# A conditioned decoder block on one core: the opening's w_ada in two sets, and the second norm in the order of need

## The chip, the core and the metric

The kernel runs on one core of one Trainium2 chip. A core has a matrix engine (TensorE, in the profile PE, with its weight loads as PEld), a vector engine (VectorE, DVE), a scalar engine (ScalarE, ACT), GpSimd (POOL) and a queue engine (SyncE, SP) that issues most DMAs here. The metric is the time of one execution on the device in microseconds (us), lower is better; the time before is the median of three runs.

## The reference

One decoder block on 256 tokens of width 2048, all in 32-bit floats. A condition vector `c` is turned by a large matrix `w_ada` (2048 x 12288) into six modulation vectors; two of them shift and scale the first norm, two the second one. Three matter here:

```python
mod = c_act @ w_ada[l] + b_ada[l]
sh1, sc1, g1, sh2, sc2, g2 = [m[:, None, :] for m in jnp.split(mod, N_MOD, axis=-1)]
h = rms_norm(x, norm_mix_g[l]) * (1.0 + sc1) + sh1
proj = h @ w_in[l]                       # u, q, k, v, ga, gb
...
x = x + g1 * (merged @ w_out[l])
h2 = rms_norm(x, norm_mlp_g[l]) * (1.0 + sc2) + sh2
x = x + g2 * (jnp.square(jax.nn.relu(h2 @ w_ff1[l])) @ w_ff2[l])
return rms_norm(x, norm_final_g)
```

Between `proj` and `merged` lie a state-space branch and an attention branch, which the change doesn't touch.

## The kernel before

**Products in three parts.** Each large product is made from split operands: a 32-bit value is cast to a shorter form (`hi`, on ACT) and the rest of it (`lo = src - hi`, on DVE) is kept beside it; three matrix products (hi x hi, hi x lo, lo x hi) are added up. `split` (lines 135 to 142) emits the cast and the subtraction and notes both in `self.done`, as a pair (subtraction, cast). It is used for the weights, which come through `stream`, and for the activations.

**The weight stream.** `stream` (lines 143 to 156) loads one tile of 128 rows and 1024 columns (512 KB) into one of seven buffers `wraw`, splits it into `whi` and `wlo`, and hands it to the product. A buffer comes free when the subtraction has read it; SP's next load hangs on that. The same seven buffers serve the tiles of `w_ada`: `ada_first` (lines 275 to 305) multiplies such tiles on PE, with outputs named `adap` and `adac`, for the first columns of the two vectors of the first norm, and `ada_job` (lines 307 to 329) multiplies them on DVE (line 323, called a modulation job here) for all others.

**Queues and order.** A planner places the instructions on each engine's queue by a priority and a simulated time line; each queue then runs strictly in its order. `high_priority` lifts what is written inside it, `hot()` most of all; `issue_after(i)`, here `after(i)`, puts what follows behind the instruction `i` on the same engine; `pin` keeps the order of the program. `self.gates` is a list of pairs: each next weight tile of the stream takes one from it, and its subtraction goes behind the first of the pair, its cast behind the second.

**The opening.** The first norm's activations `ah` and `al` are made in pairs of 128-row blocks by `make_h1` (line 419): a multiplication by the norm on DVE, scale and shift on ACT into `htmp`, then a split. The first product (`gemm_t`, line 158, for the query columns) runs over four weight rows, 0 to 3; rows 0 and 1 need the first pair of `ah`, rows 2 and 3 the second. The second pair needs its own columns of `w_ada`: four tiles for the scale, four for the shift, which `second` (line 929) loads and multiplies. It is called as `mid` from `gemm_t` in front of row 2, so that on PE all eight totals stand behind row 1. Each set of four ends in a round trip: PE `adap`, ACT copy, PE `adac`, a small DVE sum.

**The second norm.** The output projection runs by `gemm_h` (line 219): its second column half first finishes the tokens 0 to 127 (half 0), then the held products for the tokens 128 to 255 (half 1). As each half is done, `norm2` (line 1176) runs: `add1` adds the product to the residual on DVE (line 1159 and 1160) and squares it on ACT; then come the sum, `rstd` (a square root on ACT and small DVE steps), `scale2` for two column blocks (DVE, line 1172), and for each block four transposes on PE (line 1190, output `trh`), scale and shift on ACT (line 1194, into the one buffer `htmp`), and a split into `mh` and `ml`. All of it is in `hot()`.

The next product, the first of `w_ff1` (call of `gemm_h` at line 1293), has eight weight tiles, 0 to 7; tiles 0 to 3 use block 0 of the norm, tiles 4 to 7 block 1. Tiles 0 to 3 lie in `whi` and `wlo`, 4 and 5 in `wVT`, 6 and 7 in `wQT`. It takes half 0 through all eight tiles, and then half 1. The list `turns=(((6, 3),), ())` puts the products of half 0 from tile 6 on behind `self.turned[3]`, the last transpose of half 1. The gates of the eight tiles are

```python
self.gates = [(None, None)] + [(scaled[0], None)] * 2 + [(scaled[0], roots[0])] * 3 + [(h0, roots[0])] * 2
```

with `scaled[t]` the first `scale2` of half t, `roots[t]` its square root and `h0` the subtraction of half 0's second block. Behind this product six modulation jobs are forced, after `h1` (the last subtraction of half 1); the others are handed out at a rate `RM` for each step of a weight stream, over three further groups of eight steps.

Of the kernel before, what the change touches and what calls it, by code (L numbers as in the profile page):

```python
# [55 lines left out]
RSS = .43  # L56
RPA = .65
RWO = .45
RM = .45
NP = 4  # L60
TW = 9
TF = 3
# [12 lines left out]
class Kern:  # L75
# [82 lines left out]
    def gemm_t(self, src, kts, c0, xh, xl, koff=0, mid=None):  # L158
        nc = self.nc
        banks = [self.bank(f"pt{b}") for b in range(4)]  # L160
        n = len(kts)
        for i, (kt, hi, lo) in enumerate(self.stream(src, kts, c0)):
            kx = kt - koff
            if mid and i == n // 2:
                mid()
            for blk in range(8):
                o = banks[blk // 2][:, (blk % 2) * S:(blk % 2 + 1) * S]
                c = slice(blk * P, (blk + 1) * P)
                st, sp = i == 0 and blk % 2 == 0, i == n - 1
                nc.tensor.matmul(o, hi[:, c], xh[:, kx, :], start=st, stop=False, skip_group_check=True)  # L170
                nc.tensor.matmul(o, hi[:, c], xl[:, kx, :], start=False, stop=False, skip_group_check=True)  # L171
                self.mm = nc.tensor.matmul(o, lo[:, c], xh[:, kx, :], start=False, stop=sp, skip_group_check=True)  # L172
        return banks
# [101 lines left out]
    def ada_first(self, j, half, done):  # L275
        nc = self.nc
        n = 2 * (1 - j) + half
        st = {}

        def load(i):  # L280
            w = st[i] = self.wp.tile([P, 1024], F32, name="wraw", tag="wraw", bufs=7)
            with self.after(self.last):
                ld = nc.sync.dma_start(w, self.a["wan"][j, half, i])
            if self.early:
                self.last = ld

        def total(i):
            w = st.pop(i).rearrange("p (k n) -> p k n", k=4)
            if i == 0:
                st["p"] = self.aux("adap")  # L290
            p = st["p"][:, 0:256]
            with self.after(None if self.early else self.mm):
                for k in range(4):
                    q = 32 * k
                    nc.tensor.matmul(p[q:q + 32, :], self.cz[:, 4 * i + k, :], w[:, k, :], start=i == 0,
                                     stop=i == 3, tile_position=(0, q), skip_group_check=True)
# [555 lines left out]
    def body(self):  # L852
# [73 lines left out]
            self.ssm_params()  # L926
            self.bias_prep()

        def second():
            with self.tc.high_priority(offset=OF1):  # L930
                for ld, tot in modn(1):
                    ld()
                    tot()
                self.make_h1(range(2, 4), A1, B1)
        self.early = False
        self.qk = self.slot("S1", [P, 2, 8, S], name="qk")
        self.v = self.slot("SV", [P, 2, 1024], name="v")
# [64 lines left out]

        def qkvu(which, g0, g1):
            kts = range(groups[g0][0], sum(groups[g1]))
            mid = second if (which, g0) == (0, 0) else (lambda: need(g1)) if g1 > g0 else None
            need(g0)
            if which < 2:
                qk_evac(which, self.gemm_t(win, kts, 1024 + 1024 * which, self.ah, self.al, mid=mid), g0)
            elif which == 2:
                v_evac(self.gemm_n(win, kts, 3072, self.ah, self.al), g0)  # L1010
            elif which == 4:
                g_evac(self.gemm_t(win, kts, 4096, self.ah, self.al, mid=mid), g0)
            else:
                u_evac(self.gemm_t(win, kts, 0, self.ah, self.al), g0)
# [127 lines left out]
        for cg in range(2):  # L1142
# [11 lines left out]
            def add1(t):  # L1154
                with self.hot():
                    for b in (2 * t, 2 * t + 1):
                        c = slice(cg * 1024 + (b % 2) * 512, cg * 1024 + (b % 2) * 512 + 512)
                        tmp = xs[:, t, c]
                        self.pin(v.tensor_mul(tmp, banks[b], g1t["t"][:, c]))
                        self.pin(v.tensor_add(x1[:, t, c], x1[:, t, c], tmp))  # L1160
                        nc.scalar.activation(tmp, x1[:, t, c], AF.Square,
                                             accum_out=sq[:, t * 4 + cg * 2 + b % 2:t * 4 + cg * 2 + b % 2 + 1])

            if cg == 0:
# [8 lines left out]

        scaled, roots = {}, {}

        def norm2(t):
            add1(t)
            with self.hot():
                ss = self.col(f"ss2{t}", 1)
                self.pin(v.reduce_sum(ss, sq[:, 4 * t:4 * t + 4], axis=AX.X))  # L1180
                rs2[t] = self.rstd(ss, 1, f"r2{t}")
                roots[t] = self.sq_last
                tk = slice(t * P, (t + 1) * P)
                scaled[t] = [scale2(c, t) for c in range(2)][0]
                for c in range(2):
                    p = self.tmp("trh")
                    h = self.big.tile([P, 4, P], F32, name="htmp", tag="htmp", bufs=1)
                    for k in range(4):
                        kt = 4 * c + k
                        self.turned[2 * t + c] = nc.tensor.transpose(  # L1190
                            p[:, k * P:(k + 1) * P], xs[:, t, kt * P:(kt + 1) * P], self.ident)
                    for k in range(4):
                        kt = 4 * c + k
                        nc.scalar.activation(h[:, k], p[:, k * P:(k + 1) * P], AF.Identity,
                                             scale=A2[:, kt:kt + 1], bias=B2[:, kt:kt + 1])
                    last = self.split(mh[:, 4 * c:4 * c + 4, tk], ml[:, 4 * c:4 * c + 4, tk], h)
            return last

        h0 = norm2(0)
        next(parts)  # L1200
        h1 = norm2(1)
        self.gates = [(None, None)] + [(scaled[0], None)] * 2 + [(scaled[0], roots[0])] * 3 + [(h0, roots[0])] * 2

        g2b = self.slot("S3", [P, D], name="g2b")

# [84 lines left out]
        for g in range(NP):  # L1290
            part = self.slot(("S4", "T", "SV", "S5")[g], [P, 8, S], name="part")
            if g == 0:
                halves = self.gemm_h(w1, range(0, 8), 0, mh, ml, self.homes(4, ("VT", "QT")), 8,
                                     turns=(((6, 3),), ()))
                for t in range(2):
                    banks = next(halves)
                    for b in (2 * t, 2 * t + 1):
# [7 lines left out]
            if g == 0:  # L1305
                self.gates = []
                self.agate = h1
                for job in range(6):
                    if self.lanes["ada"][0]:
                        self.lanes["ada"][0].pop(0)()  # L1310
                self.agate = None
# [65 lines left out]
```

## Time and profile before

| what | us |
|---|---|
| median of 3 runs | 1417.61 (1416.76 to 1420.15) |
| profiled execution | 1415.01 |
| its span, first to last instruction | 1412.9 |
| PE idle in the span | 42.1 |

The span is read from the profile, in which each time is counted from the span's start. A row of the timeline gives start, duration, engine, line, operation, output<-inputs, shape and count, and in brackets how long the engine was idle before it and what ended that. Matrix products are pipelined, so one starts before the one ahead of it has ended.

### The profile page before, as it was taken

How to read it: one execution, taken by the hardware profiler on the slowest of the kernel's cores; microseconds unless marked ns; L12 is line 12 of the kernel's file. 1: busy time of each engine (PE TensorE's matmuls, PEld its weight loads, DVE VectorE, ACT ScalarE, POOL GpSimd, SP SyncE). 2: the span in 40 equal slices, each digit the busy share in tenths (PEclk: the TensorE clock that was granted, in tenths of full speed). 3: DMA queues.
4: the chain of work that ended last, by engine and by line, in shares of the span. 5: the costliest groups of instructions: out<-in, count | busy, mean ns of one | idle time of the engine just before them, and what ended most of it. 6: DMA issues, size and time to landing. Idle time of an engine off the chain costs nothing. (4 is left out here: it accounts for less than half of the span.)

```text
span 1412.9 us, 23391 instructions
## 1 busy us (share of the span) xinstructions
PE 1370.8 (97%) x9258; PEld 1221.4 (86%) x9258; DVE 1054.7 (75%) x1502; ACT 705.7 (50%) x937; POOL 40.8 (3%) x94
## 2 busy tenths in 40 slices
PE   7889999999999999999899999999999999999996
PEld 5779899899999999988788888888888888888885
DVE  5688989986799888978786776777676555555676
ACT  4444343366464843445555564545463544635444
POOL 1000000320000300000000000000000000000000
PEclk9999999999999999999999999999999999999998
DMA  9999987597457988797597677777767556465551
GB/s 340 368 381 351 327 295 243 164 296 243 150 190 250 320 305 294 285 349 283 181 324 262 196 263 242 246 251 278 255 221 265 184 191 195 174 203 192 182 205 60
DMA packets 113293, 353.19 MB, mean 250 GB/s; under 512 B 12080, under 2 KB 12096, under 8 KB 113056
## 3 DMA queue, kind: packets, MB, share of 16 engines
q1 hardware_dynamic: 110384, 347.13, 70.6%
q0 software_dynamic: 2800, 4.58, 1.1%
q8 instruction: 72, 1.18, 0.3%
q14 instruction: 37, 0.30, 0.1%
HBM read 347.27 MB, written 2.29 MB: 247 GB/s over the span
## 5 line engine op out<-in xcount | busy, mean ns | idle before, releaser
L137 ACT CAST whi<-wraw 128x1024 fp32r<-128x1024 f32 x443 | 461.3, 1051 | 550.8 <-PE pn L268 173.4
L139 DVE TENSOR_TENSOR wlo<-wraw,whi 128x1024 fp32r<-128x1024 f32 x443 | 537.7, 1222 | 256.0 <-ACT whi L137 254.2
L198 PE MATMUL pw<-mh,whi 128*128 128x512 f32 x896 | 311.3, 396 | 1.0 <-DVE part L1303 0.5
L170 PE MATMUL pt<-ah,whi 128*128 128x256 f32 x896 | 252.0, 288 | 9.9 <-ACT whi L137 6.8
L171 PE MATMUL pt<-ah,whi 128*128 128x256 f32 x896 | 250.8, 286 | 0.0
L200 PE MATMUL pw<-mh,wlo 128*128 128x256 f32 x896 | 242.4, 280 | 0.0
L172 PE MATMUL pt<-ah,wlo 128*128 128x256 f32 x896 | 238.7, 285 | 2.7 <-DVE wlo L139 2.5
L323 DVE SCALAR_TENSOR_TENSOR wraw<-wraw,cb 128x1024 f32<-128x1024 f32 x176 | 213.3, 1219 | 0.0
L268 PE MATMUL pn<-whi,ff 128*128 128x512 f32 x512 | 199.3, 389 | 0.0
L267 PE MATMUL pn<-whi,ff 128*128 128x512 f32 x512 | 198.6, 390 | 0.0
L198 PEld LDWEIGHTS pw<-mh,whi 128*128 128x128 f32 x896 | 165.4, 188 | 37.3 <-DVE part L1303 0.8
L269 PE MATMUL pn<-wlo,ff 128*128 128x512 f32 x512 | 185.3, 389 | 0.0
L170 PEld LDWEIGHTS pt<-ah,whi 128*128 128x128 f32 x896 | 172.5, 194 | 13.3 <-ACT whi L137 8.7
L171 PEld LDWEIGHTS pt<-ah,whi 128*128 128x128 f32 x896 | 173.2, 194 | 0.4
L200 PEld LDWEIGHTS pw<-mh,wlo 128*128 128x128 f32 x896 | 168.8, 188 | 4.7 <-DVE wlo L139 0.4
L172 PEld LDWEIGHTS pt<-ah,wlo 128*128 128x128 f32 x896 | 165.5, 193 | 4.2 <-DVE wlo L139 3.9
L267 PEld LDWEIGHTS pn<-whi,ff 128*128 128x128 f32 x512 | 96.1, 188 | 20.1 <-issue 0.2
L269 PEld LDWEIGHTS pn<-wlo,ff 128*128 128x128 f32 x512 | 96.1, 188 | 20.0
L268 PEld LDWEIGHTS pn<-whi,ff 128*128 128x128 f32 x512 | 96.1, 188 | 19.6
L1273 DVE TENSOR_TENSOR y<-y,pn 128x512 f32<-128x512 f32 x48 | 30.8, 682 | 14.9 <-PE pn L269 14.9
L267 PE MATMUL pn<-whi,mh 128*128 128x512 f32 x96 | 37.6, 392 | 0.0
L268 PE MATMUL pn<-whi,mh 128*128 128x512 f32 x96 | 37.4, 390 | 0.0
(400 smaller groups left out, 1655.4 us busy)
## 6 DMA issues: line engine op xcount, KB each, us to landing
wraw<-in_w_ff_dram SPq DMA_DIRECT2D x256, 512.0 KB, 4.7
wraw<-in_wat_dram SPq DMA_DIRECT2D x176, 512.0 KB, 5.8
wraw<-in_w_in_dram SPq DMA_DIRECT2D x128, 512.0 KB, 5.2
wraw<-in_w_out_dram SPq DMA_DIRECT2D x32, 512.0 KB, 6.3
wraw<-in_wan_dram SPq DMA_DIRECT2D x16, 512.0 KB, 8.7
wraw<-in_w_proj_attn_dram SPq DMA_DIRECT2D x16, 512.0 KB, 6.3
wraw<-in_w_proj_ssm_dram SPq DMA_DIRECT2D x16, 512.0 KB, 6.2
wraw<-in_w_glu_dram SPq DMA_DIRECT2D x8, 512.0 KB, 5.5
```

The source lines that it names most:

```text
L137: h = self.nc.scalar.copy(hi, src)
L139: s = self.nc.vector.tensor_sub(lo, src, hi.bitcast(F32))
L170: nc.tensor.matmul(o, hi[:, c], xh[:, kx, :], start=st, stop=False, skip_group_check=True)
L171: nc.tensor.matmul(o, hi[:, c], xl[:, kx, :], start=False, stop=False, skip_group_check=True)
L172: self.mm = nc.tensor.matmul(o, lo[:, c], xh[:, kx, :], start=False, stop=sp, skip_group_check=True)
L198: nc.tensor.matmul(banks[b], hi[:, c], x2[:, k0 + k].rearrange("p h s -> p (h s)"), start=i + k == 0, stop=False, skip_group_check=True)
L200: self.mm = nc.tensor.matmul(banks[b][:, 0:S], lo[:, c], x2[:, k0 + k, 0, :], start=False, stop=i == n - 1 and k == 1, skip_group_check=True)
L267: nc.tensor.matmul(o, xh[:, kx, tk], hi[:, c], start=q == 0, stop=False)
L268: nc.tensor.matmul(o, xl[:, kx, tk], hi[:, c], start=False, stop=False)
L269: self.mm = last = nc.tensor.matmul(o, xh[:, kx, tk], lo[:, c], start=False, stop=q == n - 1)
L323: v.scalar_tensor_tensor(w, w, 1.0, self.cb[:, (i % 2) * 1024:(i % 2 + 1) * 1024], op0=OP.mult, op1=OP.mult, accum_out=pc[:, i:i + 1])
L1273: v.tensor_add(d, d, banks[b])
```

## The change

In the opening, `mid` may now be a dictionary from the row to a function. `second` is called twice: in front of row 1 it loads and multiplies the four tiles of the scale, and row 1's first product of each block goes behind the last of them; in front of row 2 it does the four of the shift and makes the pair. A gate then holds row 3's cast and subtraction behind the pair's. In the second norm, `norm2` is cut in two: its first part goes as far as the eight transposes, and `piece(c)` makes scale, shift and split of one block. Half 0's second block is now written behind half 1's `add1`, by `turn()`. The gates of tiles 5 to 7, the turn (tile 5 in place of 6), the number of forced jobs (four in place of six) and `RM` (0.55 in place of 0.45) change with it.

```diff
-RM = .45
+RM = .55
@@ gemm_t
-            if mid and i == n // 2:
+            turn = None
+            if isinstance(mid, dict):
+                turn = mid[i]() if i in mid else None
+            elif mid and i == n // 2:
                 mid()
...
-                nc.tensor.matmul(o, hi[:, c], xh[:, kx, :], start=st, stop=False, skip_group_check=True)
+                with self.after(turn):
+                    nc.tensor.matmul(o, hi[:, c], xh[:, kx, :], start=st, stop=False, skip_group_check=True)
@@ body
-        def second():
+        rest = modn(1)
+
+        def second(i):
             with self.tc.high_priority(offset=OF1):
-                for ld, tot in modn(1):
+                for ld, tot in rest[4 * i:4 * i + 4]:
                     ld()
                     tot()
+                if i == 0:
+                    return self.adap
                 self.make_h1(range(2, 4), A1, B1)
+                self.gates = self.done[-1:]
...
-            mid = second if (which, g0) == (0, 0) else (lambda: need(g1)) if g1 > g0 else None
+            mid = {1: lambda: second(0), 2: lambda: second(1)} if (which, g0) == (0, 0) else (lambda: need(g1)) if g1 > g0 else None
...
-        def norm2(t):
+        def norm2(t, turn):
             add1(t)
+            turn()
             with self.hot():
                 ss = self.col(f"ss2{t}", 1)
                 self.pin(v.reduce_sum(ss, sq[:, 4 * t:4 * t + 4], axis=AX.X))
                 rs2[t] = self.rstd(ss, 1, f"r2{t}")
                 roots[t] = self.sq_last
+                scaled[t] = [scale2(c, t) for c in range(2)][0]
+                trh = []
+                for c in range(2):
+                    trh.append(self.tmp("trh"))
+                    for k in range(4):
+                        kt = 4 * c + k
+                        self.turned[2 * t + c] = nc.tensor.transpose(
+                            trh[c][:, k * P:(k + 1) * P], xs[:, t, kt * P:(kt + 1) * P], self.ident)
+
+            def piece(c):
...
-        h0 = norm2(0)
+        piece0 = norm2(0, lambda: None)
+        h00 = piece0(0)
         next(parts)
-        h1 = norm2(1)
-        self.gates = [(None, None)] + [(scaled[0], None)] * 2 + [(scaled[0], roots[0])] * 3 + [(h0, roots[0])] * 2
+        h01 = []
+        piece1 = norm2(1, lambda: h01.append(piece0(1)))
+        h01 = h01[0]
+        piece1(0)
+        h1 = piece1(1)[0]
+        self.gates = [(None, None)] + [(scaled[0], None)] * 2 + [(scaled[0], roots[0])] * 2 + [(h01[0], h00[1])]
+        self.gates += [(scaled[1], self.square), (scaled[1], roots[1])]
...
-                                     turns=(((6, 3),), ()))
+                                     turns=(((5, 3),), ()))
...
-                for job in range(6):
+                for job in range(4):
```

`self.square` is the last square of `add1`. `piece(c)` holds the old lines of scale, shift and split for one block and returns `self.done[-1]`, its pair of subtraction and cast.

More of the change, by code (lines that the diff above doesn't have):

```diff
@@ L294, in total @@
                     q = 32 * k
-                    nc.tensor.matmul(p[q:q + 32, :], self.cz[:, 4 * i + k, :], w[:, k, :], start=i == 0,
-                                     stop=i == 3, tile_position=(0, q), skip_group_check=True)
+                    self.adap = nc.tensor.matmul(p[q:q + 32, :], self.cz[:, 4 * i + k, :], w[:, k, :], start=i == 0,
+                                                 stop=i == 3, tile_position=(0, q), skip_group_check=True)
             if i == 3:
@@ L1160, in add1 @@
                         self.pin(v.tensor_add(x1[:, t, c], x1[:, t, c], tmp))
-                        nc.scalar.activation(tmp, x1[:, t, c], AF.Square,
+                        self.square = nc.scalar.activation(tmp, x1[:, t, c], AF.Square,
                                              accum_out=sq[:, t * 4 + cg * 2 + b % 2:t * 4 + cg * 2 + b % 2 + 1])
@@ L1182, in norm2 @@
                 roots[t] = self.sq_last
+                scaled[t] = [scale2(c, t) for c in range(2)][0]
[7 more added lines that the diff above has]
+            def piece(c):
                 tk = slice(t * P, (t + 1) * P)
-                scaled[t] = [scale2(c, t) for c in range(2)][0]
-                for c in range(2):
-                    p = self.tmp("trh")
+                with self.hot():
                     h = self.big.tile([P, 4, P], F32, name="htmp", tag="htmp", bufs=1)
@@ L1189, in norm2 @@
                         kt = 4 * c + k
[L1190 to L1194, printed above, removed]
-                                             scale=A2[:, kt:kt + 1], bias=B2[:, kt:kt + 1])
-                    last = self.split(mh[:, 4 * c:4 * c + 4, tk], ml[:, 4 * c:4 * c + 4, tk], h)
-            return last
-        h0 = norm2(0)
-        next(parts)
-        h1 = norm2(1)
-        self.gates = [(None, None)] + [(scaled[0], None)] * 2 + [(scaled[0], roots[0])] * 3 + [(h0, roots[0])] * 2
+                        nc.scalar.activation(h[:, k], trh[c][:, k * P:(k + 1) * P], AF.Identity,
+                                             scale=A2[:, kt:kt + 1], bias=B2[:, kt:kt + 1])
+                    self.split(mh[:, 4 * c:4 * c + 4, tk], ml[:, 4 * c:4 * c + 4, tk], h)
+                return self.done[-1]
+            return piece
+        piece0 = norm2(0, lambda: None)
+        h00 = piece0(0)
+        next(parts)
+        h01 = []
[5 more added lines that the diff above has]
+        self.gates += [(scaled[1], self.square), (scaled[1], roots[1])]
         g2b = self.slot("S3", [P, D], name="g2b")
```

## The prediction

> **What bounds the kernel now.** I read the page first: span, busy shares, the slices.
>
> ```profile
> span 1412.9 us, 23391 instructions
> PE 1370.8 (97%) x9258; PEld 1221.4 (86%) x9258; DVE 1054.7 (75%) x1502; ACT 705.7 (50%) x937; POOL 40.8 (3%) x94
> DMA  9999987597457988797597677777767556465551
> ```
>
> TensorE (PE) is busy for all but 42.1 us of the span, so nearly all that an ordering change can win lies in those 42.1 us. The DMA digits say that the first six slices of 35 us are at 9 or more, the later ones seldom: the kernel has a supply-bound opening and a TensorE-bound rest. The windows show where each begins.
>
> ```profile
> 28.00:32.00 4.00, 4.00 (x30) 3.32 (x29) 2.16 (x3) 1.12 (x3) 0.57 (x1) 1.00 1.11 404
> 32.00:36.00 4.00, 3.51 (x47) 2.36 (x45) 0.00 (x0) 0.37 (x1) 0.00 (x0) 1.00 0.62 214
> 36.00:40.00 4.00, 2.34 (x35) 1.03 (x34) 0.32 (x2) 0.37 (x1) 0.00 (x0) 1.00 0.95 326
> 43.00:49.80 6.80, 4.42 (x19) 4.13 (x20) 6.80 (x10) 2.04 (x3) 0.00 (x0) 0.50 0.99 389
> 75.40:112.00 36.60, 31.57 (x235) 29.01 (x236) 31.91 (x44) 20.50 (x30) 0.00 (x0) 1.00 0.97 373
> 263.50:678.00 414.50, 414.50 (x3644) 393.69 (x3641) 348.66 (x496) 222.62 (x309) 34.91 (x72) 1.00 0.77 267
> 684.00:700.00 16.00, 12.53 (x59) 9.98 (x58) 9.18 (x18) 7.11 (x18) 0.00 (x0) 1.00 0.49 180
> 750.00:1413.00 663.00, 651.56 (x3249) 551.02 (x3247) 430.03 (x544) 328.84 (x413) 0.58 (x1) 0.99 0.63 214
> ```
>
> Columns: length, busy time of PE, weight loads, DVE, ACT, POOL, granted clock, DMA share, GB/s. From 263.5 to 678 PE never stops, and after 750 it idles 11.4 us of 663; whatever is won ahead of such a stretch reaches the end of the span. Between 75.4 and 112 PE idles 5.0 us with DMA at 0.97. What the casts wait for there is told by the waits of 50 to 165 us:
>
> ```profile
> ACT whi L137 <- DMA wraw<-in_w_in_dram: 42.7, 24, 3.3
> ```
>
> 24 casts stood 42.7 us for weights in flight. So a TensorE that leaves the opening early meets data that isn't there: the opening is worth what it moves the *loads*, not what it takes from PE's holes. Those holes, and the two vector engines in them:
>
> ```profile
> 29.62 0.38 PE L170 MATMUL pt<-ah,whi 128*128 128x256 f32 x1
> 33.03 1.93 PE L295 MATMUL adap<-wraw,tz 128*32 128x256 f32 x32
> 38.67 0.64 PE L295 MATMUL adap<-wraw,tz 128*32 128x256 f32 x8 [1.17 <-DMA wraw<-in_wan_dram]
> 43.43 1.22 PE L170 MATMUL pt<-ah,whi 128*128 128x256 f32 x4 [3.03 <-ACT ah L137]
> 46.59 0.58 PE L170 MATMUL pt<-ah,whi 128*128 128x256 f32 x1 [1.94 <-ACT whi L137]
> 20.28 13.78 SPq L283 DMA_DIRECT2D wraw<-in_wan_dram  x6
> 44.14 0.33 SPq L132 DMA_DIRECT2D wraw<-in_w_in_dram  x1
> 40.70 1.09 ACT L428 ACTIVATE htmp<-xt,B,A 128x256 f32<-128x256 f32 x2 [0.95 <-DVE B L890]
> 41.81 1.04 ACT L137 CAST whi<-wraw 128x1024 fp32r<-128x1024 f32 x1
> 42.76 0.61 ACT L137 CAST ah<-htmp 128x512 fp32r<-128x512 f32 x1
> 42.89 1.23 DVE L139 TENSOR_TENSOR wlo<-wraw,whi 128x1024 fp32r<-128x1024 f32 x1 [2.29 <-ACT whi L137]
> 44.03 1.22 DVE L323 SCALAR_TENSOR_TENSOR wraw<-wraw,cb 128x1024 f32<-128x1024 f32 x1
> 46.32 0.69 DVE L139 TENSOR_TENSOR ah<-htmp,ah 128x512 fp32r<-128x512 f32 x1
> ```
>
> All four tiles of the scale half are there at 33.03 (32 products, no wait), but stand behind weight row 1, whose products begin at 29.62. Six w_ada issues crawl from 20.28 to 34.06, each for a buffer. Then the second pair's cast (42.76) stands behind that of weight row 3, and its low part (46.32) behind that row's low part and two modulation jobs of line 323: from cast end 43.37 to 47.01 nothing on the chip needed 3.6 us except this order.
>
> The second place is the norm, PE first, then DVE, then ACT:
>
> ```profile
> 678.66 1.06 PE L1190 MATMUL trh<-ident,xs 128*128 128x128 f32 x8 [0.62 <-DVE xs L1172]
> 685.25 0.50 PE L229 MATMUL pn<-whi,mh 128*128 128x512 f32 x1 [0.94 <-DVE mh L139]
> 692.64 0.39 PE L229 MATMUL pn<-wVT,mh 128*128 128x512 f32 x1
> 692.86 0.39 PE L230 MATMUL pn<-wVT,mh 128*128 128x512 f32 x1
> 695.78 1.06 PE L1190 MATMUL trh<-ident,xs 128*128 128x128 f32 x8 [2.53 <-DVE xs L1172]
> 682.24 2.35 DVE L139 TENSOR_TENSOR wVT<-wraw,wVT 128x1024 fp32r<-128x1024 f32 x2
> 684.51 0.69 DVE L139 TENSOR_TENSOR mh<-htmp,mh 128x512 fp32r<-128x512 f32 x1
> 687.48 0.69 DVE L139 TENSOR_TENSOR mh<-htmp,mh 128x512 fp32r<-128x512 f32 x1 [2.29 <-ACT mh L137]
> 688.09 0.68 DVE L1159 TENSOR_TENSOR xs<-pn,g1b 128x512 f32<-128x512 f32 x1
> 688.69 2.35 DVE L139 TENSOR_TENSOR wQT<-wraw,wQT 128x1024 fp32r<-128x1024 f32 x2
> 695.15 0.88 DVE L1172 TENSOR_SCALAR xs<-x,r21s 128x512 f32<-128x512 f32 x2
> 682.43 0.62 ACT L137 CAST mh<-htmp 128x512 fp32r<-128x512 f32 x1
> 683.69 0.61 PE L228 MATMUL pn<-whi,mh 128*128 128x512 f32 x2
> ```
>
> Two holes count: 0.94 us, where PE waits for the first low part, and 2.53 us, where it waits for the second half's scaled rows. The output projection is finished at 683.69 (PE is already in the next product), yet DVE takes up the second half's residual only at 688.09: it stood 2.29 us for a cast it needn't have waited for, then put two weight splits between.
>
> **The opening.** Nothing is removed; eight loads, eight totals and two round trips stay, and only their place changes. The four scale totals move ahead of weight row 1, the four shift totals stay behind it.
>
> - The scale totals need 1.93 us (the x32 row), and can start when row 0 is done: at 29.6, 3.4 us sooner (row 1's products follow them now). On PE this is a swap, price 0, if the loads have landed. The bound if not: one landing late, 1.3 us (0.524 MB at the 404 GB/s of 28 to 32).
> - Those totals hand four buffers back 3.4 us sooner. The DMA engines had room there: (1 - 0.62) x 4 + (1 - 0.95) x 4 = 1.7 us of idle. The last shift tile needn't wait for its buffer any more; row 1 ends near 29.6 + 1.9 + 3.4 = 34.9, and four totals behind it, 1.93 us at least, end near 36.8, not 39.31.
> - The new gate, `gates = done[-1:]`, holds row 3's cast and split behind the pair's. Queued behind that cast on ACT are only later weight casts, behind the split on DVE the line 323 jobs; these release buffers for SP. By the old spacings (last total to `htmp` 40.70 - 39.31 = 1.39 us, 1.09 us for that) `htmp` is there at 39.3, the pair cast by 39.9, its low part done by 40.6 (was 47.01), row 3 cast by 41.0 and split by 42.2 instead of 44.12. Behind that end SP issued at 44.14. So the loads restart **2.0 us** sooner, rounded up from 1.9.
>
> PE wins about 6 us here (6.4 at the low part), and gives back all but the loads' part while it waits between 75 and 112. I take -2.0; the ends are 0 (the later supply absorbs it) and -6.1, the sum 1.17 + 3.03 + 1.94 of the three holes.
>
> [...] The row 43.00:49.80 has a clock of 0.50 behind holes of 3.03 and 1.94 us, while 684:700, with a hole of 2.53, has 1.00. [...]
>
> **The norm.** Counts stay: 16 transposes, 16 scalings, four casts and splits.
>
> - First hole. Tile 5 of w_ff1 is now gated behind the low part of the first half's second block, so one of the two wVT splits (2.35 / 2 = 1.17 us) leaves the place ahead of 684.51. The low part then ends by 684.0, and ACT too has one weight cast less ahead of its own; PE needs it after two products, at 684.3. -0.94.
> - Second hole. `add1(1)` now stands ahead of the second block's split, and tiles 6 and 7 are gated behind the scaled rows. From 688.09 to 695.15 the chain took 7.06 us; less the splits, which sat there from 688.69 to 690.96 (2.27 us), it is 4.8. Starting at 684.1 it reaches the scaling at 688.9, or 689.6 if the moved low part (0.69 us) falls inside. PE takes up the first scaled block 0.63 us behind that (695.15 to 695.78), so at 690.2. By `turns` it is at the transposes one tile sooner (six products, 0.22 to 0.23 us apart in the rows, 1.36 us): at 693.25 - 0.94 - 1.36 = 690.95. The rows wait for PE: -2.53, with 0.7 us to spare. If tiles 3 and 4 are split inside the chain, 2.35 us, a hole of 1.6 is left.
> - What is late next: the second block of the first half, which its cast and split now reach behind `add1(1)`. It is needed from the fifth tile on, at 683.69 + 4 x 1.36 = 689.1; cast by about 686 and split by 688.5, 0.6 to spare. Tile 5, split behind it, is needed at 692, tiles 6 and 7 at 693.4 and 694.7, splits from 689.6 on reach them.
> - No DMA is added; two modulation jobs fewer are forced behind the norm (2 x 1.22 us of DVE time), and `RM` hands them out over 24 steps: 0.55 x 24 = 13.2 for 12 left, before 0.45 x 24 = 10.8 for 10. Price 0; the cover is PE's backlog of products, and the bound is the one such hole there is:
>
> ```profile
> 749.22 0.50 PE L198 MATMUL pw<-mh,whi 128*128 128x512 f32 x1 [0.51 <-DVE part L1303]
> ```
>
> Norm: -3.5, ends -1.9 and -4.1 (with the 0.62 hole, which nothing here touches).
>
> **Sum.** -2.0 - 3.5 = -5.5 us: span 1412.9 to 1407.4, and the profiled execution (1415.01, so 2.1 around the span) to 1409.5. It stood 2.6 under the median of 1417.61; the median becomes **1412.1**. About 0.3%, 4.3 us, can be told from no change, so this forecast stands just beyond that edge, at 1413.4.
>
> **The rivals.**
> 1. *The supply takes all of the opening.* DVE and DMA are both nearly full from 50 to 165, and a load that starts sooner may only wait longer in line. For it: 42.7 us of waits; against it: the DMA idle that is filled was real. Norm alone: 1414.1.
> 2. *The planner keeps its order.* `turn()` changes the order in the program, a simulated time line the one in the queues. If DVE still stands for the second block's cast (the 2.29 us) and only the 2.27 us of splits go, the transposes run at 695.78 - 2.27 = 693.5 with one tile less done ahead of them: 2.27 - 1.36 = 0.9 us gained. 1417.6 - 2.0 - 0.9 = 1414.7.
> 3. *Slower: the earlier turn.* `turns` forces the transposes one tile forward. If the scaled rows come no sooner, the transposes run at 695.78 as now with a tile less behind PE: 1.36 us lost, whatever was saved at 685. It decides from the point where the scaling starts later than 695.15 - 1.36 = 693.8. With an opening that brings nothing: 1417.6 + 1.4 = 1419.0. Against it: the 2.29 us stand and the 2.27 us of splits are both taken out of that chain.
> 4. *The clock stays up.* If the opening's hole falls to some 2.5 us, the clock stays at 1.00 as it did from 684 to 700, the halved stretch of 6.8 us gives 3.4 us back, and if PE, not the supply, sets the pace after it, the median is 1412.1 - 3.4 = 1408.7. Against it: the 42.7 us of cast waits. [...]
>
> **Chances.** Forecast 0.50, rival 1 0.17, rival 2 0.13, rival 3 0.08, rival 4 0.12. The forecast's own spread, about 1.5 us to each side, lets a sixth of its 0.50 fall inside the 0.3% edge. Faster: 0.42 + 0.12 = 0.54; same: 0.08 + 0.17 + 0.13 + 0.01 = 0.39; slower by over 0.3%: 0.07, since rival 3 alone stays within the edge and needs one more new wait of 3 us for it. The range, 1407.8 to 1417.5, leaves out most of rival 3 and the lower edge of rival 4.
>
> **What would show it.** Right: a last `adap` ending near 36.8, the low part of `ah` before row 3's `wlo`, and the SP issue that stood at 44.14 near 42.2; no idle before L229 and none over 0.5 us before the second eight transposes; the first `xs<-pn` of the second half on DVE ahead of 685. Wrong: the cast waits of 50 to 165 growing by as much as the opening gained (rival 1); a weight split between the residual's two products (rival 2); a hole over 3 us before the transposes (rival 3); a clock of 1.00 from 43 to 50 together with less PE idle up to 165 (rival 4).

## The result and the profile after

| | before | after |
|---|---|---|
| median, us | 1417.61 (4 runs) | 1408.16 (4 runs, 1407.12 to 1411.44) |
| profiled execution, us | 1415.01 | 1411.44 |
| its span, us | 1412.9 | 1409.3 |

The ratio is 0.9941, with a 95% interval of 0.9926 to 0.9956: the change takes 8.4 us off, between 6.2 and 10.5. (The two medians, each of four runs, lie 9.5 us apart; the four of before are one more than ahead of the prediction, with the same median. Here and below, a gain in us is the ratio's distance from 1, taken of the median of before.) The two profiled executions differ by 3.6 us only: the first is shorter than the four of before in the table, and the second is the longest of the four after. This pair alone tells too little; the experiments below therefore bring two more profiles of the changed kernel and one more of the kernel before.

First the page of the changed kernel: span, busy time by engine, and DMA's busy tenths in 40 slices of 35 us.

```profile
span 1409.3 us, 23394 instructions
PE 1371.2 (97%) x9258; PEld 1221.7 (87%) x9258; DVE 1056.0 (75%) x1502; ACT 706.4 (50%) x937; POOL 40.9 (3%) x94
DMA  9999987597457988887687677777767556565551
```

PE's idle time fell from 42.1 to 1409.3 - 1371.2 = 38.1 us. The work is the same, and so are the DMA digits of the first sixteen slices.

**The opening after.** The timeline of the changed kernel, in the order PE, ACT, DVE and SP's queue (start, duration, engine, line, operation, and in brackets the idle time before it):

```profile
30.33 1.93 PE L299 MATMUL adap<-wraw,tz 128*32 128x256 f32 x32
35.70 2.24 PE L299 MATMUL adap<-wraw,tz 128*32 128x256 f32 x32
41.12 0.73 PE L174 MATMUL pt<-ah,whi 128*128 128x256 f32 x4 [2.09 <-ACT ah L137]
39.33 1.09 ACT L432 ACTIVATE htmp<-xt,B,A 128x256 f32<-128x256 f32 x2 [0.95 <-DVE B L894]
40.45 0.62 ACT L137 CAST ah<-htmp 128x512 fp32r<-128x512 f32 x1
40.97 1.04 ACT L137 CAST whi<-wraw 128x1024 fp32r<-128x1024 f32 x1
41.10 0.69 DVE L139 TENSOR_TENSOR ah<-htmp,ah 128x512 fp32r<-128x512 f32 x1 [1.87 <-ACT ah L137]
42.05 1.23 DVE L139 TENSOR_TENSOR wlo<-wraw,whi 128x1024 fp32r<-128x1024 f32 x1 [0.26 <-ACT whi L137]
43.30 0.33 SPq L132 DMA_DIRECT2D wraw<-in_w_in_dram  x1
```

The scale totals now stand ahead of weight row 1, and the pair's cast (40.45) and low part (41.10) ahead of those of row 3 (40.97, 42.05). Two holes of 3.03 and 1.94 us have become one of 2.09, in front of the second pair's first product. The low part of `ah` ends at 41.79, 5.2 us sooner than before. But SP's queue, at 43.30, restarts only 0.84 us sooner than its old 44.14. So the windows are read as well. First the kernel before, then the changed one, and its clock (columns: length, busy time of PE, weight loads, DVE, ACT, POOL, granted clock, DMA share, GB/s):

```profile
28.00:60.00 32.00, 24.88 (x212) 21.37 (x211) 18.31 (x29) 10.76 (x17) 0.57 (x1) 0.89 0.96 358
```

```profile
28.00:60.00 32.00, 28.74 (x254) 24.66 (x252) 19.96 (x31) 12.47 (x19) 0.58 (x1) 1.00 1.00 383
40.00:52.00 12.00, 10.88 (x88) 10.69 (x89) 10.09 (x14) 7.10 (x10) 0.00 (x0) 1.00 1.00 380
159.10:165.93 6.83, 5.27 (x24) 5.28 (x25) 6.83 (x10) 3.14 (x3) 0.00 (x0) 0.50 0.91 326
258.09:264.92 6.83, 5.83 (x94) 5.49 (x96) 6.05 (x9) 4.26 (x7) 0.00 (x0) 0.50 0.57 176
```

From 28 to 60 us 25 GB/s more were moved in this execution: 25 x 32 = 0.80 MB, or 2.1 us at 383 GB/s. The further profiles below don't repeat that (experiment 6 has them side by side). PE is 3.9 us busier in that stretch, and has to wait for weights again behind it, where the kernel before had no wait of this kind from 50 to 75:

```profile
56.54 0.38 PE L174 MATMUL pt<-ah,whi 128*128 128x256 f32 x1 [0.51 <-ACT whi L137]
61.14 0.50 PE L271 MATMUL pn<-whi,ah 128*128 128x512 f32 x1 [1.16 <-ACT whi L137]
```

The last two rows of the windows tell where this execution lost most of what it had won: its clock stood at 0.50 for 6.83 us from 159.10 and for 6.83 us from 258.09. In the profile of before the two halved stretches there were 3.41 us long (from 162.47 and 261.45). By this clock, an estimate, each 3.41 us of it cost up to half of that, 1.7 us, of PE's work.

**The norm after,** PE, then DVE, and one hole further on:

```profile
679.18 1.06 PE L1199 MATMUL trh<-ident,xs 128*128 128x128 f32 x8 [1.17 <-DVE xs L1181]
691.10 1.06 PE L1199 MATMUL trh<-ident,xs 128*128 128x128 f32 x8
683.89 0.68 DVE L139 TENSOR_TENSOR mh<-htmp,mh 128x512 fp32r<-128x512 f32 x1
684.49 0.68 DVE L1168 TENSOR_TENSOR xs<-pn,g1b 128x512 f32<-128x512 f32 x1
687.33 0.69 DVE L139 TENSOR_TENSOR mh<-htmp,mh 128x512 fp32r<-128x512 f32 x1
687.94 1.22 DVE L139 TENSOR_TENSOR wVT<-wraw,wVT 128x1024 fp32r<-128x1024 f32 x1
690.47 0.88 DVE L1181 TENSOR_SCALAR xs<-x,r21s 128x512 f32<-128x512 f32 x2
745.00 0.39 PE L204 MATMUL pw<-mh,wlo 128*128 128x256 f32 x1 [1.04 <-DVE wlo L139]
```

The residual starts right behind the first low part. One low part and one weight split still fall inside the chain, and yet the scaled rows come in time, if only just: PE took up the first of them 0.63 us after their scaling began in the profile of before (695.15 to 695.78), and it does so here (690.47 to 691.10). The second eight transposes show no bracket, the 2.53 us are gone, and so are the 0.94 before the first product. Longer than before: the hole before the first transposes is 1.17 (was 0.62), and the one near 745 is 1.04 (was 0.51 at 749.22).

### The profile page after: what moved, and what is told of

It reads as the page before. It is cut to its first block, busy times and chain, and to the rows that moved or that the text cites. A ratio compares the mean times of both kernels' runs of the same rounds, so it can differ in the third digit from the quotient of the medians.

```text
span 1409.3 us, 23394 instructions
## 1 busy us (share of the span) xinstructions
PE 1371.2 (97%) x9258; PEld 1221.7 (87%) x9258; DVE 1056.0 (75%) x1502; ACT 706.4 (50%) x937; POOL 40.9 (3%) x94
## 4 chain that ended last, share of the span: by engine, by line
PE 86%; DMA 6%; DVE 5%; ACT 1%; issue 1%; SPq 0%; DVEq 0%; ACTq 0%
PE pw L202 14%; PE pn L271 10%; PE pn L273 10%; PE pn L272 10%; PE pt L174 9%; PE pt L176 9%; PE pt L175 9%; PE pw L204 7%; DMA wraw<-in_w_in_dram 3%; DVE wlo L139 2%; DVE wraw L327 1%; PE pn L233 1%; PE pn L234 1%; PE pn L232 1%; DMA wraw<-in_wat_dram 1%
```

## Experiments

"Before" in each comparison is the kernel before, run on the same chip in between: medians of 1415.84 us (runs 1 to 4), 1416.27 (5 to 8) and 1416.42 (9 to 12).

### 1. The opening alone

Only the opening's part of the diff (two sets, `after(turn)`, the gate); the norm stays as it was.

> The kernel before with the new opening alone (two sets, row 1 behind the first set, the gate on row 3); the norm as before. Theory A (the opening is worth the loads' head start, some 2.0 to 2.4 us, and what the clock adds or takes is chance of one execution): 1.5 to 3.5 us less than the kernel before, ratio 0.9975 to 0.999. Theory B (the head start is lost again at the later holes near 160 and 260 us, as in the one profile of the changed kernel): within 0.7 us. Theory C (the old opening's two holes cost more than its one profile showed): 4.5 us or more, ratio under 0.9968.

Median 1412.92 us, ratio 0.9982 (0.9972 to 0.9991): -2.5 us (-4.0 to -1.3), as theory A has it; B and C lie outside the interval. The profile of this run holds something that neither profile of the kernel before shows. Its timeline at the second transposes, and its windows:

```profile
694.00 1.82 PE L1199 MATMUL trh<-ident,xs 128*128 128x128 f32 x8 [2.53 <-DVE xs L1181]
```

```profile
690.74:694.15 3.41, 0.88 (x6) 0.45 (x5) 2.18 (x9) 0.93 (x3) 0.00 (x0) 1.00 0.57 201
694.15:697.56 3.41, 3.41 (x13) 3.02 (x13) 0.41 (x2) 2.12 (x5) 0.00 (x0) 0.50 0.00 0
```

The same 2.53 us hole that left the clock at 1.00 in the two profiles of before (684 to 700 us in the first, 690 to 700 in run 4) is followed here by 3.41 us at half clock; the eight transposes take 1.82 us, not 1.06. So a hole's length doesn't settle the clock. In run 1 PE was busy for 0.88 and idle for 2.53 of the 3.41 us ahead of the halved stretch, so the whole hole lay in them. In the first profile of before the halved stretches up to 265 us begin at 22.52, 43.00, 162.47 and 261.45, which is 6, 35 and 29 times 3.413 us apart; 191 such steps behind 43.00, near 694.95, the same hole is cut in two:

```profile
691.55:694.96 3.41, 1.70 (x8) 1.08 (x6) 2.18 (x9) 1.65 (x5) 0.00 (x0) 1.00 0.75 267
```

Here PE was idle for 1.7 us, and from 694.96 to 698.37 the clock was 1.00. That the outcome hangs on where a hole falls is the author's estimate from these two windows and not shown; the idle time alone doesn't order the cases either, since in the first profile of the changed kernel 1.44 us of it from 155.69 to 159.10 were followed by half clock.

### 2. The norm alone

The norm's part of the diff with `RM`, the gates and the earlier `turns`; the opening stays as it was.

> The kernel before with the new norm alone (order, gates of tiles 5 to 7, turn at tile 5, four forced jobs, RM 0.55). Theory A: 3.0 to 4.0 us less (the two holes of 0.94 and 2.53 us), ratio 0.9972 to 0.9979; in its profile no idle before L229 and none over 0.5 us before the second transposes. Theory B: the norm carries the whole measured gain, 7 us or more, ratio under 0.995. Theory C: 3.0 to 4.0 us, as A.

Median 1412.16 us, ratio 0.9973 (0.9962 to 0.9984): -3.8 us (-5.4 to -2.3), inside theory A's 3.0 to 4.0, and theory B's 7 lies outside the interval. The timeline has neither of the norm's two holes any more, and the opening's two are as large as ever:

```profile
43.24 1.22 PE L174 MATMUL pt<-ah,whi 128*128 128x256 f32 x4 [3.73 <-ACT ah L137]
46.40 0.58 PE L174 MATMUL pt<-ah,whi 128*128 128x256 f32 x1 [1.94 <-ACT whi L137]
678.14 1.06 PE L1194 MATMUL trh<-ident,xs 128*128 128x128 f32 x8 [0.99 <-DVE xs L1176]
```

The two parts alone make -2.5 and -3.8, in sum -6.3 us; the changed kernel beside them (run 3) has -7.5 (-9.3 to -5.8). The 1.2 us between lie inside the intervals.

### 3 and 4. The changed kernel again, and the kernel before against itself

> The changed kernel again. If the two halves simply add up (A): the sum of the gains of the two kernels run with it, within 1.5 us, some 5 to 6 us. If the first measurement was representative (C): 8 to 9.5 us. If spread between executions comes from the TensorE clock, its spans follow its mean clock by about 1.4 us for each 0.001; if from the loads, they don't.

> The kernel before against itself: ratio 1.000 within its interval. A second profile of it: if the clock is halved for 3.4 or 6.8 us behind the holes at 43, 160 and 260 us at random (A), the halved stretches differ in place or length from those of the first profile (3.4 at 22.5, 6.8 at 43.0, 3.4 at 162.5, 3.4 at 261.5) and the span differs by half of the difference; if they are fixed by the program, they are the same.

The changed kernel: 1407.90 us, 0.9947 (0.9934 to 0.9959), -7.5 us: within 1.5 us of the sum of the parts; theory C's 8 to 9.5 isn't excluded. The kernel before against itself: 0.9998 (0.9990 to 1.0007). Its second profile has the halved stretches of the first in the same lengths and within 0.3 us in the same places (3.41 us at 22.21, 6.83 at 42.69, 3.41 at 162.16 and at 261.15; from 28 to 60 us the clock is 0.89 in both), which by itself speaks for stretches fixed by the program. The changed kernel speaks against it: its three profiles differ, with 6.83 us from 258.09 in the first, 3.41 from 256.80 in run 3 and 6.83 from 257.43 in run 10. Whether the clock makes the scatter between executions stays open: for each 0.001 of the mean granted clock the time falls by 0.15 us over the five executions of run 3, by 1.65 over the six of run 10 and by 0.74 over the 23 of before (runs 1 to 4), where 1.4 was expected.

These runs give the traces that the first pair lacked. In the table each PE instruction of a trace is set against its counterpart in the trace of run 4, and the median of the differences in start is taken in three stretches (us, negative is sooner; "norm" is the third less the second).

| profile | 120 to 140 | 500 to 660 | from 1000 on | norm |
|---|---|---|---|---|
| before, first profile | -0.3 | -0.4 | 0.0 | +0.5 |
| changed, first profile | -2.7 | -0.5 | -3.5 | -3.0 |
| changed, run 3 | -3.3 | -4.3 | -7.5 | -3.2 |
| changed, run 10 | -1.8 | -1.5 | -5.1 | -3.6 |
| opening alone, run 1 | -2.1 | -2.7 | -0.4 | +2.4 |
| norm alone, run 2 | -0.1 | -1.3 | -4.6 | -3.3 |

The norm's step is much the same in every execution that has the new norm. The opening's is not: 1.8 to 3.3 us at 120, and between there and 500 it is raised by up to 1.0 or cut by up to 2.2; the traces differ there in what the clock does near 160 and 258 (near 160, 6.83 us at half clock in the first profile of the changed kernel and 3.41 in that of before; near 258, 3.41 in run 3 and 6.83 in the other two of the changed kernel). The +2.4 of run 1 are mainly its halved stretch at 694: 3.41 us at a clock of 0.50 are, as an estimate, 1.7 us of PE's work. Run 4 is a low mark for the old norm: the four other traces with it (before, runs 1, 5 and 6) have +0.5, +2.4, +1.3 and +0.9 there, so that the new norm's -3.0 to -3.6 are rather too small a figure for it.

### 5. The two sets without the gate

Against run 1:

```diff
                 self.make_h1(range(2, 4), A1, B1)
-                self.gates = self.done[-1:]
```

> The kernel before with the two sets of w_ada tiles alone, without the gate on row 3. Theory A (the opening is worth what the loads gain, here the DMA idle of 32 to 40 us, 1.7 us): 1 to 2 us less than the kernel before; the first scale total on PE near 30, the last shift total ending near 38, but the pair's cast still behind row 3's and its low part still behind modulation jobs. Rival (the gate is what counts): within 0.7 us.

Median 1415.46 us, 0.9990 (0.9982 to 0.9999): -1.4 us, between -2.5 and -0.1. That is theory A's size, and the rival's 0.7 isn't excluded. DVE's timeline around the pair, and PE's product that waits for it:

```profile
40.65 1.23 DVE L139 TENSOR_TENSOR wlo<-wraw,whi 128x1024 fp32r<-128x1024 f32 x1 [2.60 <-ACT whi L137]
41.80 1.22 DVE L327 SCALAR_TENSOR_TENSOR wraw<-wraw,cb 128x1024 f32<-128x1024 f32 x1
44.09 0.69 DVE L139 TENSOR_TENSOR ah<-htmp,ah 128x512 fp32r<-128x512 f32 x1
44.83 0.58 PE L175 MATMUL pt<-ah,whi 128*128 128x256 f32 x1 [2.41 <-DVE ah L139]
```

Without the gate the pair's low part stands behind row 3's split and two modulation jobs of line 327 again, though the totals are sooner. The loads restart at 41.91 us, 2.2 us sooner than in the first profile of before, and yet PE stands only 0.3 us sooner from 120 on than in run 4.

### 6. The gate without the two sets

Against the kernel before:

```diff
                 self.make_h1(range(2, 4), A1, B1)
+                self.gates = self.done[-1:]
         self.early = False
```

> The kernel before with the gate on row 3 alone; all eight totals still behind row 1. Theory A: PE wins some 3 us at the pair's low part, but row 3's split, on which the loads hang, comes 0.5 to 1 us later than 44.1; since the loads set the pace up to 160 us, within 1 us of the kernel before. Rival (PE sets the pace): 2.5 us or more less.

Median 1414.67 us, 0.9990 (0.9981 to 0.9999): -1.4 us, between -2.7 and -0.1; within 1 us was expected, 2.5 or more by the rival. Row 3's split did not come later (42.69, by 0.20 sooner than in the first profile of before). In its timeline the one line of the gate already turns the two holes into one, and makes the later waits longer:

```profile
41.76 1.19 PE L174 MATMUL pt<-ah,whi 128*128 128x256 f32 x4 [2.09 <-ACT ah L137]
74.05 0.50 PE L271 MATMUL pn<-whi,ah 128*128 128x512 f32 x1 [2.03 <-ACT whi L137]
```

Against run 4, PE stands 4.0 us sooner between 40 and 60, and 0.3 us from 120 on. That is the clearest sight of the rule that the prediction used: PE's lead out of the opening lasts only as far as the loads have one. (The profiled execution is one of the longer ones of this kernel, 1416.98 us, as is that of run 5, 1416.65; by their medians both kernels keep more.)

Side by side, SP's first issue after the pause (us), the rate of the DMAs (GB/s) over a short and a long window, and PE's place against run 4 at 120 to 140 us:

| profile | SP restarts | GB/s, 28 to 60 | GB/s, 28 to 112 | PE at 120 |
|---|---|---|---|---|
| before, first profile | 44.14 | 358 | 361 | -0.3 |
| before, run 4 | 43.67 | 360 | 358 | 0 |
| sets alone, run 5 | 41.91 | 356 | 360 | -0.3 |
| gate alone, run 6 | 43.95 | 350 | 357 | -0.3 |
| opening alone, run 1 | 44.04 | 355 | 368 | -2.1 |
| changed, first profile | 43.30 | 383 | 374 | -2.7 |
| changed, run 3 | 42.46 | 365 | 368 | -3.3 |
| changed, run 10 | 43.99 | 353 | 365 | -1.8 |

Neither the restart nor the first 32 us tell the kernels apart; the 84 us from 28 to 112 do. The loads gain only where both halves of the opening are there, and in runs 1 and 10 they gain behind 60 us. One place where PE's lead reaches them can be seen on ACT, first in run 4, then in run 1:

```profile
63.16 2.27 ACT L947 COPY qk<-pt 128x512 f32<-128x512 f32 x4 [2.41 <-PE pt L172]
65.32 1.06 ACT L137 CAST whi<-wraw 128x1024 fp32r<-128x1024 f32 x1
59.55 1.56 ACT L956 COPY qk<-pt 128x512 f32<-128x512 f32 x3 [2.44 <-PE pt L176]
60.99 1.06 ACT L137 CAST whi<-wraw 128x1024 fp32r<-128x1024 f32 x1
```

The cast of a weight stands behind copies that wait for PE's finished product. PE is sooner, so the cast is 4.3 us sooner, and SP's load that stood at 67.66 is issued at 65.77. But run 6 has this too (cast at 61.34, load at 66.11) and has lost most of it by 80 us; what lets the loads keep it with both halves is open.

### 7 and 8. The earlier turn, and the modulation jobs

The changed kernel with the transposes one tile later, and the changed kernel with the old handing out of the jobs:

```diff
-                                     turns=(((5, 3),), ()))
+                                     turns=(((6, 3),), ()))
```

```diff
-RM = .55
+RM = .45
...
-                for job in range(4):
+                for job in range(6):
```

> The changed kernel with the transposes of the second half forced at tile 6 again, as before. Theory A (the rows are now ready before PE, so the turn only shifts the transposes among products): between 0 and 1.4 us more than the changed kernel, ratio to before 0.994 to 0.996; a hole, if any, in front of the second half's first products. Rival (the earlier turn costs, as my rival 3 has it): 1 us or more less than the changed kernel, with its transposes later and no hole.

> The changed kernel with six forced modulation jobs and RM 0.45 again, as before. Theory A (the jobs lie beside PE's backlog): within 0.7 us of the changed kernel, with the hole near 745 back at 0.5 us. Rival (the forced jobs hold buffers that the next group's weights need): 1.5 us or more slower than the changed kernel, with waits for DVE or casts between 705 and 730.

The later turn: 1409.44 us, 0.9956 (0.9944 to 0.9969), as theory A has it, and not told apart from the changed kernel's 0.9947 of runs 1 to 4. The old jobs: 1408.71 us, 0.9947 (0.9933 to 0.9960), the same as the changed kernel, also as theory A has it. PE's rows at the second transposes of run 7, and at the hole near 745 of run 8:

```profile
689.82 1.04 PE L1199 MATMUL trh<-ident,xs 128*128 128x128 f32 x8
```

```profile
742.30 0.50 PE L202 MATMUL pw<-mh,whi 128*128 128x512 f32 x1 [0.51 <-DVE part L1324]
```

The transposes find their rows with either turn, so the prediction's third rival, by which the earlier turn costs 1.36 us, finds no place to arise. With the old jobs the hole near 745 is 0.51 again, not 1.04, and the 0.5 us can't be seen in the time.

### 9. The opening's hole filled

```diff
                 if i == 0:
                     return self.adap
+                dmy = self.aux("dmy")
+                with self.after(self.adac):
+                    for _ in range(12):
+                        nc.tensor.matmul(dmy[:, 0:P], self.ident, self.ident, start=True, stop=True)
```

> The changed kernel, with twelve products of the identity by itself put on PE behind the last adac of the opening, into the 2.09 us hole before the second pair's first product; nothing reads what they give. Theory A (behind the opening the supply of weights sets the pace, so a halved clock near 42 is given back in the waits of 55 to 110): the hole shrinks to some 0.5 us, the clock near 42 stays at 1.00, and the time stays within 0.7 us of the changed kernel's of the same batch. Theory B (the opening alone brought more than its loads' 2.0 us because a shorter hole leaves less half-clock time): at least 1 us less than the changed kernel, and a mean clock 0.001 higher.

> The changed kernel once more, to be compared with the other three of this batch. All theories: 0.9945 of the kernel before, within 0.0013; PE's one hole between 183 and 670 is the 3.26 us before the first rk products, and it is followed by a stretch at half clock near 257.

Filled: 1410.07 us, 0.9954 (0.9942 to 0.9966). The changed kernel beside it (run 10): 1409.13 us, 0.9946 (0.9933 to 0.9960). The filled kernel's timeline, its windows, and those of run 10:

```profile
38.46 2.92 PE L945 MATMUL dmy<-ident 128*128 128x128 f32 x24
41.14 0.72 PE L174 MATMUL pt<-ah,whi 128*128 128x256 f32 x4
```

```profile
40.00:48.00 8.00, 8.00 (x70) 8.00 (x69) 7.08 (x10) 4.88 (x8) 0.00 (x0) 1.00 0.91 343
55.00:112.00 57.00, 48.50 (x331) 43.36 (x331) 49.83 (x70) 29.27 (x40) 0.00 (x0) 1.00 0.97 370
```

```profile
40.00:48.00 8.00, 6.19 (x37) 6.00 (x38) 5.96 (x8) 3.98 (x6) 0.00 (x0) 0.79 1.02 392
55.00:112.00 57.00, 49.73 (x342) 44.56 (x341) 49.76 (x72) 29.07 (x40) 0.00 (x0) 1.00 0.98 370
```

(Each of the twelve products counts as two instructions in the row.) The hole is gone and the clock stays at 1.00 where run 10 has 0.79. PE then idles 57 - 48.5 = 8.5 us between 55 and 112, run 10 7.3. Against run 4 the filled kernel's PE stands 6.1 us sooner between 40 and 60 and 2.0 from 120 on; run 10's stands 3.8 and 1.8 sooner. So nearly all of the fuller clock's lead is given back by 120. The time is not shorter but 0.9 us longer, which the intervals don't tell from nothing, and which is a little more than the 0.7 expected. Of theory B the clock came true (0.9940 in the mean of the five executions, 0.9928 in run 10's six), the time didn't, though with this scatter the times alone don't exclude a gain of 1 us. Run 10 itself came out as expected, with one hole of 3.27 us before `rk` and half clock behind it.

### 11 and 12. A hole that the change leaves: the scan's parameters sooner

From 264 to 676 PE of the changed kernel doesn't stop, as this window of its first profile shows, so the 3.27 us hole before the `rk` products and the half clock behind it should lie on the path.

```profile
264.00:676.00 412.00, 412.00 (x3626) 391.84 (x3623) 346.93 (x489) 220.81 (x305) 35.03 (x72) 1.00 0.77 266
```

`SL` counts the empty steps before the jobs that feed those products.

```diff
-SL = 6
+SL = 5
```

> The changed kernel with SL = 5 for 6: the scan's parameter jobs are handed out one step sooner, so that the rk products stand some 40 matmuls later on PE against their inputs. Theory A (from 183 to 670 PE is the bound and the clock's halving there follows from the hole): the 3.26 us hole before rk shrinks under 1.5 us, the halved stretch near 257 goes, and the time is 2 to 5 us below the changed kernel's. Rival (the jobs only meet DVE and ACT sooner, and weight splits come late for it): new waits of PE for wlo or whi between 190 and 250, and a time within 1.5 us of the changed kernel's or above it.

> The changed kernel with SL = 4 for 6. Theory A as for SL = 5: 2 to 5 us below the changed kernel's, the hole before rk under 1.5 us. Rival: new waits for wlo or whi between 190 and 250, and a time within 1.5 us of the changed kernel's or above it.

`SL = 5` (run 11): 1407.77 us, 0.9936 (0.9923 to 0.9948). `SL = 4` (run 12): 1408.11 us, 0.9940 (0.9928 to 0.9953). Run 10 at the `rk` products, timeline and window:

```profile
257.76 0.48 PE L651 MATMUL rk<-cc,tt 64*64 64x64 f32 x4 [3.27 <-ACT tt L641]
```

```profile
257.43:264.26 6.83, 6.50 (x106) 6.16 (x108) 6.02 (x9) 3.92 (x7) 0.00 (x0) 0.50 0.67 208
```

Run 11, the same place and two others:

```profile
259.95 2.26 PE L651 MATMUL rk<-cc,tt 64*64 64x64 f32 x70
179.03 0.39 PE L176 MATMUL pt<-ah,wlo 128*128 128x256 f32 x1 [1.39 <-DVE wlo L139]
302.26 0.39 PE L174 MATMUL pt<-ah,whi 128*128 128x256 f32 x1 [1.21 <-ACT whi L137]
```

```profile
255.00:265.00 10.00, 10.00 (x214) 9.87 (x215) 9.75 (x15) 5.38 (x9) 4.09 (x9) 1.00 0.77 234
```

The hole and the halved stretch are gone, as theory A has it; but PE waits 1.39 us for a split at 179 (run 10: 0.51) and 1.21 us for a weight at 302 (run 10: none), which is the rival's kind of wait, though not between 190 and 250, where the rival put it. Run 12 loses the hole too, and has waits of 0.73, 0.76 and 1.12 us from 299 to 303, and from 303.83 to 306, behind the last one, its products take 0.41 to 0.42 us where those ahead of the waits took 0.28. The medians are 1.4 and 1.0 us below run 10's and the intervals overlap with its own: neither is shown to beat the change, and the 2 to 5 us expected did not come. The two longer waits of run 11 took some 2.1 us; the rest can't be told from the scatter of single executions. That PE, sooner by this, meets the supply is argued and not shown: run 6, with `SL = 6`, has a like wait, 1.64 us in front of 309.06, while run 3, which is further ahead there, has none. So PE doesn't always pass this stretch without a stop, and a gain made before it isn't always kept.

## Why the prediction came out as it did

The direction and the range were right, and the norm's mechanism with its size. The opening's size was nearly right, but its path to the loads was not. The time, 1408.16 for 1412.1, lies near the lower end of the range. Step by step:

- **The opening, loads restart 2.0 us sooner.** The size held, and was slightly short: -1.8, -2.7 and -3.3 us at 120 in three profiles, mean -2.6, and -2.5 in the time of the opening alone. The step that failed is the restart. In the first profile the marks were late: the last totals ended at 37.94 (36.8 expected), the pair's low part at 41.79 (40.6), SP issued at 43.30 (42.2). Run 3 nearly met them (42.46 for SP), and runs 1 and 10 issued at 44.04 and 43.99, no sooner than before, with the gain all the same; run 5 issued at 41.91 and gained 0.3 at 120. So the gain does not hang on that mark. Nor does it on the DMA's idle time of 1.7 us ahead of it, which the prediction had in its rows and didn't price: only the first profile moves clearly more from 28 to 60 us, while from 28 to 112 all with the new opening do (365 to 374 GB/s, the others 357 to 361). Runs 5 and 6 show that it takes both halves. The ends of that term, 0 and -6.1, were right to be far apart: in its trace run 6 wins 4.0 us on PE and keeps 0.3.
- **PE gives its lead back.** It did, but sooner than said: waits begin at 56 in the first profile, not between 75 and 112. That whatever is won ahead of a stretch without a stop reaches its end holds for the changed kernel's three profiles from 264 to 676; run 6's wait at 309 is a case where it doesn't. The DMA digits of the profile page have five slices at 9, not six; the sixth is an 8. Nothing hangs on it.
- **Rival 1, all is given back:** refuted by run 1 (-4.0 to -1.3). The sign named for it, longer cast waits for weights from 50 to 165 us, is no measure of it: 40.1 us in the first profile, 42.3 in run 1, 47.2 and 49.6 in runs 3 and 10, where 42.7 and 43.5 stood before. **Rival 2, the planner keeps its order:** refuted by the first `xs<-pn` of the second half at 684.49. **Rival 3, the earlier turn:** refuted by runs 2 and 7.
- **Rival 4, the clock.** Its time, 1408.7, lies closest to the measured one, but not for its reason. The clock did stay at 1.00 from 40 to 52 in the first profile; in runs 6 and 10, behind the same 2.09 us hole, it was 0.50 for 3.41 us (from 41.83 and 42.39). With the clock up, PE stood 2.7 us sooner at 120; run 10, where it was halved, has 1.8 there, and run 3 has 3.3. Run 9, which keeps it up, shows no gain. Nor do the mean clocks follow the time: run 5 has nearly that of the kernel before beside it (0.991 and 0.990), run 6 has 0.992, and both gain 1.4 us. That a hole of some 2.5 us leaves the clock at 1.00, as from 684 to 700 us in the profile of before, fell with run 1, where 2.53 us were followed by 3.41 us at half clock, and with run 10, where 2.09 us were. Behind one hole the clock is halved in one execution and not in another, and what decides it was not shown.
- **The norm, -3.5.** Right in place and size: -3.0, -3.2 and -3.6 us in three profiles, -3.8 (-5.4 to -2.3) in the time of the norm alone. The transposes stood at 691.10 where 690.95 was expected. A split did fall inside the chain and used up the 0.7 us to spare; it cost nothing since PE came no sooner. The hole before the first transposes varies without an edit that aims at it: 1.17, 1.12 and 0.64 in three profiles of the changed kernel, and 0.62 and 1.15 with the old norm (first profile, run 1). The term not seen is the clock: behind the old hole it was halved for 3.41 us in run 1, and the new norm has no such hole.
- **The sum, and where the 3.9 us lie.** Measured side by side the change is worth 7.5 us (5.8 to 9.3, run 3) and 7.6 (5.7 to 9.5, run 10), where the sum had 5.5. Of these 2 us, the two terms measured alone give 0.8 (-2.5 for -2.0, -3.8 for -3.5); the other 1.2 are inside the intervals and stay open. The rest of the 3.9 is scatter of the first two medians, which lie 9.5 us apart, and those of runs 3 and 10 only 7.9 and 7.3. The forecast for a profiled execution, 1409.5, agrees with the three of the changed kernel (1411.44, 1407.48 and 1409.75, mean 1409.56), and that is luck in part: the two of before stand 0.5 to 2.6 us below the medians of their kernel, and the three stand on average 1.2 us *above* theirs (+3.3, -0.4, +0.6). One candidate for the open part is the stretch at 694 that was halved in run 1, in neither profile of before, and that the new norm removes, by the estimate above 1.7 us each time it happens; it is argued, not shown.

## What to carry to other kernels

A hole in an engine ahead of a supply-bound stretch is worth what it moves the loads (run 6 won 4.0 us on PE there and kept 0.3 at 120). A single queue mark doesn't tell that, nor do the bytes of a window that ends too soon or of a single execution; the bytes moved over the whole supply-bound stretch did (365 to 374 GB/s with both halves of the opening, 357 to 361 without). In a stretch that one engine bounds, a chain put in the order of need is worth its holes nearly in full (3.0 to 3.6 us for holes of 0.94 and 2.53), even if one foreign instruction stays inside it. A difference of a few microseconds between two profiled executions says little: measure the effect with medians or ratios of several, and don't take one execution's distance from its median for a property of the kernel.

## What the runs showed of the hardware

- Where the clock was halved (0.50), the stretches were 3.41 us long (run 1 from 694.15), 6.83 us (run 10 from 257.43) or 10.24 us (run 5 from 40.27). They didn't always follow the same hole: 2.53 us were followed by one in run 1 and not in the two profiles of before; 2.09 us were followed by one in runs 6 and 10 and not in the first profile of the changed kernel. With the hole of 3.26 to 3.27 us before `rk` went 3.41 us of it in run 3 (from 256.80, the hole ending at 256.28) and 6.83 us in run 10 and in the first profile of the changed kernel (from 257.43 and 258.09, the hole ending at 257.76 and 259.09).
- Up to 265 us the halved stretches began whole multiples of 3.413 us apart in the first profile of each kernel: at 22.52, 43.00, 162.47 and 261.45 us before (6, 35 and 29 times), at 22.57, 159.10 and 258.09 after (40 and 29 times). What decides which holes are followed by one was not shown: 1.44 us of PE's idle time from 155.69 to 159.10 were, in the first profile of the changed kernel, and 1.7 us from 691.55 to 694.96 were not, in that of before.
